# Feed-forward: the stores of the down projection's right factors move from SyncE's DMA queue to GpSimd's

## The chip, the core and the metric

The program runs on one core of a Trainium2 chip. A core has TensorE (PE: matrix products; a weight load PEld goes beside it), VectorE (DVE), ScalarE (ACT), GpSimd (POOL) and SyncE (SP), and 16 DMA engines that move data between its on-chip memory (SBUF) and DRAM. The engines run apart from each other. Each takes its own instructions strictly in order and waits, where told, on counters that other engines and finished transfers raise. A DMA is issued by an engine as one instruction in that engine's order. Here nearly all are issued by SP, which computes nothing.

The metric is the device time of one execution in microseconds (us); less is better. It is given as the median of several runs. The profile is one further execution, recorded by the hardware.

## The reference

One inference step of a two-layer decoder in fp32. A prompt of 1024 tokens, 16 learned meta tokens and 8 x 8 sampled tokens go through together, 1104 rows of width 1024. Layer 0 is a Mamba-2 mixer and a feed-forward block, layer 1 a sliding-window attention and a feed-forward block, then a final norm. What matters here is the feed-forward block, which is there once in each layer:

```python
hn = rmsnorm(h, ffn_norm_g[layer])
h = h + (silu(hn @ w_gate[layer]) * (hn @ w_up[layer])) @ w_down[layer]   # 1024 -> 2816 -> 1024
```

## The kernel before

**Seven products for eight.** Each feed-forward product is done by Strassen's scheme in Winograd's form. Both factors are cut into 2 x 2 blocks, sums and differences of the blocks are formed, and seven block products take the place of eight. `PRODUCTS` names for each product its left factor (A11, A12, A22, S1 to S4, from the weights) and its right factor (B11, B21, B22, T1, T2, T3, N4, from the activations). Each factor is split into a high and a low part (`split_copy`, L78 to L80: ACT writes the rounded high part H, L79, and DVE the rest L, L80), and `mm` (L1489 to L1493) makes one product of three matmuls: H by xH, H by xL, L by xH.

**Up.** `up` runs over 22 slices `j` of 128 gate and up columns. Each slice has seven products of 24 matmuls (each 128 x 128 by 276 columns in layer 0, 272 in layer 1). `after_up` (L1495 to L1532) takes each finished product out of PSUM: on ACT (L1500, L1509) and on DVE (L1507, L1510, L1512, L1514, L1516, L1520), and joins them to silu(gate) times up.

**The right factors for down.** Two slices make a unit `u`, 11 in all. Each unit gives seven right factors of [128, 2, 552] in layer 0 and [128, 2, 544] in layer 1 (high and low part), which do not fit on the chip. `task` (L1534) makes a small function for each: a difference on DVE where one is needed (L1540), the split into one of three staging buffers taken in turn (L1541 to L1543: ACT's L79, DVE's L80), and a DMA that stores the staging buffer to its DRAM tile `facts[u][nm]` (L1544). That is 77 stores in each layer. The staging buffers lie in memory called `big` (layer 0) or `hN` (layer 1), two of them, and `tot`, the third; the DRAM tiles show as `f_B`, `f_T` and `f_N`, by the factor's first letter. While the up products run, one task is taken per product (L1456 and L1457); the tasks left at the end are taken during the first two products of down (L1628).

**Down.** `down` (L1568) goes through the units in chunks of two, the last of three, with seven products each, in the first chunk in the order B11, T2, T3, N4, B21, T1, B22 (`DOWN_FIRST`). `load` (L1574 to L1588) fetches the right factors back from DRAM into six buffers `bo`, as early as a buffer is free (L1585). These lie over the memory of the right factors of up: the first `bo` buffer over T2 of up, the others over T2 and T3, so that the first load waits in the instruction stream for up's last read of T2 and the second for its last read of T3. The left factors come from `prepare_down`: `source` forms S1, S3, S2 and S4 on DVE (L1131, L1134, L1138, L1141) and `factor` splits them (ACT L1149, DVE L1150). In the first product of the first chunk PE goes over unit 0 for all four row blocks, 24 matmuls, and then over unit 1. The results are added to the residual `hN` (DVE, L1639); where a lane is new they are copied to `sumX`, `sumY` or `sumZ` (ACT, L1649). The residual itself is fetched back from DRAM (`res`) into `hN` when product index 2 to 5 of the whole stage begins (L1608), over memory that the last tasks still read.

**What sets the order.** The text of the program gives each instruction a place. A planner then walks a model of the machine and lays down each engine's order once, ahead of time: what is ready first on the model is put first. SP's order thus holds weight loads (L1170 for gate and up, L1181 for down), the stores L1544, the loads L1585 and the residual's loads L1608, in the order in which they came up on the model; on the chip an instruction that isn't ready holds up all that follow it in its queue. The order of each queue around the change is planned anew when the store changes its queue.

Of the kernel before, what the change touches and what calls it, by code (L numbers as in the profile page):

```python
# [10 lines left out]
F32 = mybir.dt.float32  # L11
# [66 lines left out]
def split_copy(nc, H, L, src):  # L78
    nc.scalar.copy(H, src)  # L79
    nc.vector.tensor_tensor(L, src, H.bitcast(F32), ALU.subtract)  # L80
# [1129 lines left out]
class FeedForward:  # L1210
# [323 lines left out]
    def task(self, u, nm, at, terms=None):  # L1534


        def run():
            nc = self.nc
            if terms:
                nc.vector.tensor_tensor(at, *terms, ALU.subtract)  # L1540
            st = self.stage[self.turn % 3]  # L1541
            self.turn += 1
            split_copy(nc, st[:, 0], st[:, 1], at)  # L1543
            nc.sync.dma_start(self.facts[u][nm][:], st.bitcast(F32))  # L1544

        self.tasks.append(run)

# [936 lines left out]
```

## Time and profile before

| | |
|---|---|
| median of 3 runs | 2869.57 us (2868.34 to 2872.6) |
| the profiled execution, its own time | 2869.85 us |
| its span, first to last instruction | 2868.1 us |
| PE, DVE, ACT, POOL busy | 2760.2, 2022.5, 1222.4, 487.1 us |
| feed-forward of layer 0: stores L1544 | 1052.1 to 1489.0 us |
| the same of layer 1 | 2196.0 to 2623.7 us |
| stores L1544, by SP | 154 |

Engine rows give the busy time of each engine. A row of the timeline gives start, length, engine, line, operation and tiles, and in brackets how long the engine stood idle before it and what ended that. "issue" there means that the profile shows nothing for which the engine waited. A row of a window table gives a stretch, its length, and then for PE, PEld, DVE, ACT and POOL the busy time and the count of instructions, the granted TensorE clock (1.00 is full), the busy share of the DMA engines and the GB/s that they moved. SPq marks SP's queue: the time at which it issued, not the time of the transfer; a row with x2 or x4 runs from the first issue to the end of the last.

### The profile page before, as it was taken

What the parts mean: (1) busy time and instruction counts of PE and PEld (TensorE: products, weight loads), DVE (VectorE), ACT (ScalarE), POOL (GpSimd) and SP (SyncE); (2) the same over time, 40 slices, a digit from 0 to 9 for tenths busy, and PEclk for the clock granted to TensorE, in tenths of its full rate; (3) what the DMA queues carried; (4) which work ended last, traced back from release to release, by engine and by line L of the source; (5) the groups of instructions that cost most, each with busy time, mean ns of one, the idle gap of its engine ahead of it and who ended that gap; (6) DMA issues with size and microseconds to landing.
All of it is one profiled execution on the core that took longest, in us unless ns stands there. A gap on an engine that the chain in (4) does not pass through costs nothing. (4 is left out here: it accounts for less than half of the span.)

```text
span 2868.1 us, 51222 instructions
## 1 busy us (share of the span) xinstructions
PE 2760.2 (96%) x19990; PEld 2545.5 (89%) x19990; DVE 2022.5 (71%) x3633; ACT 1222.4 (43%) x2580; POOL 487.1 (17%) x692
## 2 busy tenths in 40 slices
PE   7999999899999899999999999998999999999998
PEld 7888989877888799999999997665998999999998
DVE  6779676647574698777768791555479777877786
ACT  4667554346442344333332243545434433433224
POOL 1455444314222100000000002332210000000000
PEclk9999999999999999999999999998999999999999
DMA  6776866565554434444468652001623443437664
GB/s 201 236 233 225 273 216 215 183 234 192 198 177 169 137 99 171 136 150 140 138 258 305 227 198 79 20 23 50 184 88 114 171 136 131 161 142 303 239 219 156
DMA packets 327009, 496.58 MB, mean 173 GB/s; under 512 B 24479, under 2 KB 222559, under 8 KB 325713
## 3 DMA queue, kind: packets, MB, share of 16 engines
q1 hardware_dynamic: 325614, 491.20, 50.5%
q8 instruction: 158, 2.59, 0.4%
q10 hardware_dynamic: 1152, 2.10, 0.2%
q14 instruction: 85, 0.70, 0.1%
HBM read 317.93 MB, written 175.30 MB: 172 GB/s over the span
## 5 line engine op out<-in xcount | busy, mean ns | idle before, releaser
L1149 ACT CAST wo<-ws 128x512 fp32r<-128x512 f32 x428 | 263.7, 620 | 546.1 <-PE wacc L1492 246.5
L1491 PE MATMUL dacc<-bo,wo 128*128 128x276 f32 (+1 forms) x1232 | 360.3, 292 | 10.3 <-DMA bo<-f_B 5.4
L1493 PE MATMUL dacc<-bo,wo 128*128 128x276 f32 (+1 forms) x1232 | 358.0, 291 | 0.0
L1492 PE MATMUL dacc<-bo,wo 128*128 128x276 f32 (+1 forms) x1232 | 357.9, 291 | 0.0
L1150 DVE TENSOR_TENSOR wo<-ws,wo 128x512 fp32r<-128x512 f32 x428 | 297.4, 698 | 69.0 <-ACT wo L1149 59.6
L73 PE MATMUL acc<-uH,wH 128*128 128x296 f32 (+1 forms) x840 | 276.5, 329 | 1.7 <-DVE th L762 1.6
L74 PE MATMUL acc<-uL,wH 128*128 128x296 f32 (+1 forms) x840 | 275.5, 328 | 0.0
L75 PE MATMUL acc<-uH,wL 128*128 128x296 f32 (+1 forms) x840 | 274.2, 326 | 0.9 <-DVE wL L156 0.9
L1491 PEld LDWEIGHTS dacc<-bo,wo 128*128 128x128 f32 x1232 | 234.4, 190 | 11.5 <-issue 10.9
L1492 PEld LDWEIGHTS dacc<-bo,wo 128*128 128x128 f32 x1232 | 234.4, 190 | 0.0
L1493 PEld LDWEIGHTS dacc<-bo,wo 128*128 128x128 f32 x1232 | 234.1, 190 | 0.0
L73 PEld LDWEIGHTS acc<-uH,wH 128*128 128x128 f32 x840 | 158.9, 189 | 16.7 <-issue 6.6
L75 PEld LDWEIGHTS acc<-uH,wL 128*128 128x128 f32 x840 | 158.8, 189 | 11.6 <-issue 2.3
L74 PEld LDWEIGHTS acc<-uL,wH 128*128 128x128 f32 x840 | 158.8, 189 | 10.6 <-issue 2.2
L585 DVE SCALAR_TENSOR_TENSOR cc<-raw,convw,cc 128x616 f32<-128x616 f32 (+1 forms) x144 | 134.3, 936 | 39.5 <-ACT cc L583 37.9
L1639 DVE TENSOR_TENSOR hN<-hN,dacc 128x544 f32<-128x544 f32 (+1 forms) x164 | 116.7, 720 | 27.9 <-PE dacc L1493 26.4
L73 PE MATMUL acc<-yH,wH 128*128 128x296 f32 (+1 forms) x360 | 122.3, 342 | 6.9 <-ACT yH L79 3.7
L2285 POOL MEMSET mask<- 128x64 f32 x1 | 0.2, 154 | 727.0 <-PE dacc L1493 727.0
L74 PE MATMUL acc<-yL,wH 128*128 128x296 f32 (+1 forms) x360 | 120.6, 336 | 0.1
L75 PE MATMUL acc<-yH,wL 128*128 128x296 f32 (+1 forms) x360 | 120.2, 335 | 0.0
L1491 PE MATMUL wacc<-N4H,wo 128*128 128x276 f32 (+1 forms) x352 | 102.7, 292 | 4.7 <-DVE hN L1504 2.4
L1149 ACT CAST wo<-sum 128x512 fp32r<-128x512 f32 x66 | 41.0, 622 | 154.3 <-PE wacc L1492 106.7
(594 smaller groups left out, 8615.3 us busy)
## 6 DMA issues: line engine op xcount, KB each, us to landing
kept<-wH SPq DMA_DIRECT2D x56, 512.0 KB
kept<-wL SPq DMA_DIRECT2D x56, 512.0 KB
ws<-ffn_w_gate SPq DMA_DIRECT2D x44, 512.0 KB
ws<-ffn_w_up SPq DMA_DIRECT2D x44, 512.0 KB
ws<-ffn_w_down SPq DMA_DIRECT2D x44, 512.0 KB
ws<-ssm_w_in SPq DMA_DIRECT2D x40, 512.0 KB
wH<-kept SPq DMA_DIRECT2D x38, 512.0 KB
wL<-kept SPq DMA_DIRECT2D x38, 512.0 KB
```

The lines of the kernel that those rows point to most:

```text
L73: nc.tensor.matmul(out, wH, xH, start=start, stop=False)
L74: nc.tensor.matmul(out, wH, xL, start=False, stop=False)
L75: nc.tensor.matmul(out, wL, xH, start=False, stop=stop)
L585: nc.vector.scalar_tensor_tensor(o, raw[:, k : k + n], w(k), o, ALU.mult, ALU.add)
L1149: nc.scalar.copy(H, src)
L1150: (low or nc.vector).tensor_tensor(L, src, H.bitcast(F32), ALU.subtract)
L1491: nc.tensor.matmul(out, wH, xH, start=start, stop=False, skip_group_check=True)
L1492: nc.tensor.matmul(out, wH, xL, start=False, stop=False, skip_group_check=True)
L1493: nc.tensor.matmul(out, wL, xH, start=False, stop=stop, skip_group_check=True)
L1639: add = lambda d, s: nc.vector.tensor_tensor(d, d, s, ALU.add)
L2285: nc.gpsimd.memset(A.mask0[:, :NS], NEG)
```

## The change

The store of a staged right factor is issued by GpSimd in place of SyncE. Nothing else is edited. The same 154 transfers move the same bytes between the same places; only the queue in which the instruction stands, and the way in which its transfer is set up, are others.

```diff
             st = self.stage[self.turn % 3]
             self.turn += 1
             split_copy(nc, st[:, 0], st[:, 1], at)
-            nc.sync.dma_start(self.facts[u][nm][:], st.bitcast(F32))
+            nc.gpsimd.dma_start(self.facts[u][nm][:], st.bitcast(F32))
```

## The prediction

> **What bounds the kernel now.** I read the page first, then busy time by stretches, then PE's timeline where it is not full, then the queue or engine that ends last there.
>
> ```profile
> span 2868.1 us, 51222 instructions
> PE 2760.2 (96%) x19990; PEld 2545.5 (89%) x19990; DVE 2022.5 (71%) x3633; ACT 1222.4 (43%) x2580; POOL 487.1 (17%) x692
> ```
>
> ```profile
> 1300.00:1400.00 100.00, 100.00 (x787) 100.00 (x786) 79.92 (x125) 39.20 (x66) 0.00 (x0) 1.00 0.46 158
> 1400.00:1500.00 100.00, 94.99 (x721) 94.39 (x720) 67.37 (x104) 39.87 (x67) 0.00 (x0) 0.97 0.55 202
> ```
>
> PE bounds it. While the up products run and stores go out, PE is full (first row), so nothing that only speeds SP's queue there can gain. The change can gain only where PE stands idle near a store. That is the turn from up to down, twice in each layer:
>
> ```profile
> 1467.52 0.29 PE L1491 MATMUL dacc<-bo,wo 128*128 128x276 f32 x1
> ...
> 1473.53 0.57 PE L1491 MATMUL dacc<-bo,wo 128*128 128x276 f32 x1 [2.79 <-DMA bo<-f_B]
> ...
> 1499.85 0.41 PE L1491 MATMUL dacc<-bo,wo 128*128 128x276 f32 x1 [2.04 <-issue]
> ...
> 2609.75 0.56 PE L1491 MATMUL dacc<-bo,wo 128*128 128x272 f32 x1 [2.62 <-DMA bo<-f_B]
> ...
> 2635.09 0.36 PE L1491 MATMUL dacc<-bo,wo 128*128 128x272 f32 x1 [2.67 <-issue]
> ```
>
> The clock is cut after some of these, which costs as well:
>
> ```profile
> 1440.00:1445.00 5.00, 5.00 (x41) 5.00 (x40) 3.63 (x6) 0.83 (x2) 0.00 (x0) 1.00 0.41 161
> ...
> 1460.00:1465.00 5.00, 4.82 (x38) 4.59 (x37) 1.79 (x3) 0.00 (x0) 0.00 (x0) 1.00 0.01 3
> ...
> 1470.00:1475.00 5.00, 2.21 (x12) 2.02 (x12) 5.00 (x9) 0.97 (x2) 0.00 (x0) 0.77 0.99 351
> 1475.00:1480.00 5.00, 5.00 (x26) 5.00 (x25) 5.00 (x9) 5.00 (x11) 0.00 (x0) 0.54 0.80 329
> ...
> 1500.00:1505.00 5.00, 5.00 (x28) 5.00 (x29) 3.81 (x7) 0.73 (x1) 0.00 (x0) 0.66 1.03 406
> ```
>
> ```profile
> 2610.00:2615.00 5.00, 5.00 (x31) 5.00 (x32) 5.00 (x10) 4.38 (x10) 0.00 (x0) 0.72 1.02 420
> ```
>
> Full clock gives 41 matmuls in 5 us, one in 0.122; half clock one in 0.245. The 26 of the fourth row mean half clock up to about 1478.6, 5.1 us after PE resumed, a loss of 2.6 us. In the same way I read losses of 1.6 us at 1500 and 1.3 us at 2610, and next to none after 2635. So the four stalls cost 5.4 + 3.6 (layer 0) and 3.9 + 2.7 (layer 1): **15.6 us in all, the most that can be won**.
>
> **Why PE waits.** SP's queue in layer 0, then the first rows of layer 1:
>
> ```profile
> 1455.82 0.39 SPq L1585 DMA_DIRECT2D bo<-f_B  x1
> 1467.64 0.32 SPq L1544 DMA_DIRECT2D f_B<-big  x1
> 1468.06 0.38 SPq L1585 DMA_DIRECT2D bo<-f_B  x1
> 1468.53 2.56 SPq L1585 DMA_DIRECT2D bo<-f_T  x4
> 1471.21 8.54 SPq L1585 DMA_DIRECT2D bo<-f_N  x2
> ...
> 1489.02 0.63 SPq L1544 DMA_DIRECT2D f_B<-big  x1
> 1489.70 1.08 SPq L1608 DMA_DIRECT2D hN<-res  x2
> ```
>
> ```profile
> 2603.78 0.52 SPq L1544 DMA_DIRECT2D f_B<-hN  x1
> 2604.39 0.56 SPq L1585 DMA_DIRECT2D bo<-f_B  x1
> ...
> 2607.50 7.20 SPq L1585 DMA_DIRECT2D bo<-f_N  x2
> ```
>
> The second load of `bo` (unit 1's B11) stands behind a store that isn't ready until 1467.6. By itself it waits only for up's last read of T3, which is over when DVE can take that product out:
>
> ```profile
> 1460.52 0.73 DVE L1512 TENSOR_TENSOR hA<-big,wacc 128x552 f32<-128x552 f32 x1 [3.60 <-PE wacc L1493]
> ...
> 1475.76 0.68 DVE L1150 TENSOR_TENSOR wo<-ws,wo 128x512 fp32r<-128x512 f32 x1
> ...
> 1477.01 0.68 DVE L1150 TENSOR_TENSOR wo<-ws,wo 128x512 fp32r<-128x512 f32 x1
> ...
> 1499.03 1.36 DVE L1639 TENSOR_TENSOR hN<-hN,dacc 128x552 f32<-128x552 f32 x2
> ```
>
> ```profile
> 2613.07 0.68 DVE L1150 TENSOR_TENSOR wo<-ws,wo 128x512 fp32r<-128x512 f32 x1
> ...
> 2634.27 3.46 DVE L1639 TENSOR_TENSOR hN<-hN,dacc 128x544 f32<-128x544 f32 x5 [0.55 <-DMA hN<-res]
> ```
>
> So the store holds the loads for 7.5 us, in which the DMA engines are idle (share 0.01 above). The second stall of each layer ends when DVE can add the fourth product to the fetched residual (L1639 at 1499.03 and 2634.27, PE 0.8 us later); the residual's load was issued at 1489.70 into full DMA engines and took 9.3 us.
>
> **The change, part by part.** *Removed from SP*: 154 issues of 0.32 to 0.52 us and their waits. In up they lie beside a full PE: 0.
>
> *Added on POOL*: 154 issues. No row shows a DMA issued by POOL. Lower bound 0.32 us (SP's rows); upper bound 1.63, the longest single POOL instruction on the chain of waits:
>
> ```profile
> 2122.20 1.63 POOL tot L2211
> ```
>
> ```profile
> L2285 POOL MEMSET mask<- 128x64 f32 x1 | 0.2, 154 | 727.0 <-PE dacc L1493 727.0
> ```
>
> I take 1 us, between the two. POOL has nothing to do for 727 us around layer 0's stores, so nothing is queued behind them; in layer 1 it has only two tiny memsets for the final norm. Cost on the path 0, at either end. What a slower landing could delay is the reuse of a staging buffer three tasks later, which rival C prices.
>
> *First stall, layer 0.* The second load goes at about 1460.5 and the four behind it follow. Their size:
>
> ```profile
> bo<-f_B SPq DMA_DIRECT2D x33, 552.0 KB
> ...
> hN<-res SPq DMA_DIRECT2D x4, 1104.0 KB
> ```
>
> Five of 0.565 MB at 351 GB/s take 8 us, so all are in by 1469 and PE's first product ends 48 x 0.122 after 1467.52, at 1473.4, not at about 1479.2 (24 x 0.122 at mixed clock after 1473.53, as above). But what is late next? The second product needs S2's low parts, and these come from DVE, which is busy 5.00 of 5 us from 1470 to 1480: unit 0's is done at 1476.4, unit 1's at 1477.65. DVE's chain starts with the end of up and doesn't wait for the loads, so it does not move. Eight matmuls can run before the last of these and 40 after it: end at 1477.65 + 4.9 = 1482.6, plus a cut of the clock, since PE stands idle some 3 us again. The four stalls above lost 0 to 2.6 us by it, 1.4 in the mean; so 1484.0 against 1479.2 + 5.9 = 1485.1. **Gain 1.1 us of the 5.4** (bounds -0.1 to 2.5).
>
> *First stall, layer 1.* PE's first product ended at about 2614.1 (the `f_N` row ends its wait there), the second at 2620.0. Afterwards: unit 1's low part at 2613.7, plus 4.9, plus 1.4: 2620.0. **Gain 0** (bounds -1.2 to 1.4).
>
> *Second stalls.* The residual's load no longer has a store of 0.63 us before it, and 2.8 MB of loads have left the DMA engines 7 us sooner. Bounds of its landing: at the soonest its issue plus its own 1.13 MB at 351 GB/s, 1489.7 + 3.2 = 1492.9; at the latest as before, 1499.0. DVE adds 0.8 us later. I take half of the 7 us: it lands at 1495.5, DVE's add is there at 1496.3, and PE, which ends the fourth product at 1484.0 + 2 x 5.9 = 1495.8, stands for 0.5 us, too short for a cut: **gain 3.1 us of 3.6**. In layer 1 the same step brings the landing to 2630.8, ahead of PE at about 2632: **gain 2.7** (bounds of both: 0 to all).
>
> Sum: 1.1 + 0 + 3.1 + 2.7 = 6.9 us. Against the profiled execution (2869.85 us, 1.75 of it outside the span) that makes 2863.0; it stands 0.3 above the median of 2869.57. **Predicted: 2862.7 us**, 0.24% faster, own range 2857 to 2867, from the bounds of the two first stalls and a part of the two second ones.
>
> The Trainium skill has a rule against this change ("DMA: Bandwidth & Descriptors", Issuing engines are not separate DMA queues): DMAs of all issuing engines run on the same 16 engines, and another issuer saves only sequencer issue time, usually small. By that rule alone the result is 2869.6; the row at 1467.64 speaks for more, as SP there lost a wait of 11 us ahead of ready loads, not an issue of 0.32.
>
> **Rivals.** *A, nothing moves* (2868 to 2871): DVE takes the place of the first waits, and the residual still lands late, because stores and loads now share the DMA engines side by side from 1478 on. For it: share 0.80 to 1.03 from 1470 on. Against: the idle DMA time at 1460.
>
> *B, all is won* (2869.6 - 15.6 = 2854.0): the planner, with another queue in its model, puts DVE's S2 ahead. For it: the order is planned anew. Against: S2's inputs are the same, and DVE is full there.
>
> *C, slower: late staging buffers.* Landing through POOL is so much later that the split three tasks on waits, and DVE and ACT with it.
>
> ```profile
> 1435.65 1.61 SPq L1544 DMA_DIRECT2D f_T<-big  x2
> ...
> 1441.73 0.32 SPq L1544 DMA_DIRECT2D f_B<-big  x1
> ```
>
> ```profile
>   ACT big L79: 6.5, 5
>   ACT tot L79: 3.8, 2
> ```
>
> The tightest reuse is 6.1 us from store to store, of which the two passes of the split take 1.5 (0.73 each, like the row at 1460.52): a store may take 4.6 us to land. ACT already waited for stores 7 times in layer 0 while PE was full. The same engines must take a finished product out of PSUM within one product of 24 x 0.122 = 2.9 us, a pass included, so PE stops from a landing of 4.6 + 2.2 = 6.8 us on. At 7.5 us each of the 20 units after the first ones would cost 0.7, 14 us in all: 2877 with the 6.9 won; at 8.5 us 2897. The Trainium skill names a cause ("SBUF — State Buffer", Who interferes with whom): descriptors written by GpSimd are held up while VectorE runs a two-port operation. By it nothing would be lost here, since it excepts operations with two tensor inputs, and every DVE row above is one; no run here shows it yet.
>
> **How the numbers follow.** Chances: forecast 0.46, A 0.23, B 0.14, C 0.17. What this kernel's times can tell apart is about 0.2%, 5.7 us, so faster means below 2863.8. Of the forecast's own range six tenths lie below that, 0.28; with B faster is 0.42. The other 0.18 and A make same 0.41. C is slower, 0.17. Range: the forecast and A whole, B from just above its price, C up to its nearer price: 2855 to 2877, which leaves out most of B and the far half of C.
>
> **What would show it.** Right: the second `bo` load issued near 1460; PE's first idle stretch moved from the middle of the first product to the start of the second, waiting for `wo` from DVE; no PE stall when the residual lands; POOL busy with about 154 issues. Wrong: ACT's waits for `f_` stores grown to many us and PE below full between 1050 and 1450 (C); the 2.0 and 2.7 us stalls still there (A); PE full through both turns (B).

## The result, and the profile after

The changed kernel takes 2881.32 us in the median of 7 runs (2877.14 to 2890.01), the kernel before 2869.51 (7 runs, 2868.29 to 2872.71). The ratio is 1.0040, 95% interval 1.0026 to 1.0053: **slower by 11.8 us, 0.4%**. Forecast were 2862.7 us and a range of 2855 to 2877, so the sign and the range were wrong.

The profiled execution of the changed kernel is its longest run, 2890.01 us. Its page begins:

```profile
span 2888.2 us, 51263 instructions
PE 2774.8 (96%) x19990; PEld 2557.4 (89%) x19990; DVE 2023.2 (70%) x3633; ACT 1220.9 (42%) x2580; POOL 577.0 (20%) x846
```

**Where the time went.** Four places divide the span: ACT's first and last copy out of an up product in each layer (L1500), and the first matmul `pS` of the attention (L1077). Before, then after (start of the first and of the last of each group):

```profile
L1500 ACT COPY big<-wacc x19: 612/620/624, 1063.7 to 1446.6; 128x552 f32<-128x552 f32 x19
L1500 ACT COPY hN<-wacc x19: 609/613/616, 2206.8 to 2583.0; 128x544 f32<-128x544 f32 x19
...
L1077 PE MATMUL pS<-cmask_sb,tot x18: 165/250/250, 1717.6 to 1742.3; 128*128 128x1 f32 x16, 128*80 128x1 f32 x2
```

```profile
L1500 ACT COPY big<-wacc x19: 608/619/623, 1069.4 to 1452.4; 128x552 f32<-128x552 f32 x19
L1500 ACT COPY hN<-wacc x19: 607/612/615, 2219.3 to 2595.4; 128x544 f32<-128x544 f32 x19
...
L1077 PE MATMUL pS<-cmask_sb,tot x18: 165/250/251, 1727.5 to 1752.2; 128*128 128x1 f32 x16, 128*80 128x1 f32 x2
```

Up takes 382.9 us before and 383.0 after in layer 0, and 376.2 and 376.1 in layer 1: nothing is lost there. From the last copy of up to `pS` (below: turn 0) it is 271.0 before and 275.1 after; from the last copy in layer 1 to the end of the span (turn 1) 285.1 and 292.8. That is 4.1 + 7.7 = **11.8 us in the two turns** of this profile. That it equals the difference of the medians is in part chance: in a second profile of the same kernel, below, the turns are longer by 6.7 us, since fewer stalls there are followed by half clock. What the profiled run is longer by beside the turns (5.7 us ahead of the first up copy, 2.6 in the attention) belongs to that run: in the second profile the attention takes 487.0 us, less than the 489.2 before.

**In up the stores are free.** Windows of the changed kernel inside up, and the answer of its trace on the store's line L1544 (durations in ns, minimum, median, maximum):

```profile
1300.00:1400.00 100.00, 100.00 (x787) 100.00 (x785) 77.94 (x121) 40.16 (x67) 8.53 (x16) 1.00 0.43 138
...
2500.00:2600.00 100.00, 100.00 (x801) 100.00 (x800) 76.56 (x120) 39.53 (x65) 12.09 (x19) 1.00 0.44 150
```

```profile
L1544 POOL DMA_DIRECT2D f_B<-big x23: 531/531/562, 1058.8 to 1494.1; - x23
L1544 POOL DMA_DIRECT2D f_B<-hN x23: 667/676/695, 2209.2 to 2636.3; - x23
...
  ACT tot L79: 0.6, 3
  ACT hN L79: 0.2, 1
```

PE is full. One issue costs POOL 0.53 us in layer 0 and 0.68 in layer 1, and ACT waited four times for a store, 0.8 us together. A list of the DMA issues gives the time from issue to landing as a median of 3.0 to 4.6 us.

**In the turns PE now stops three times, not twice.** PE's rows with idle time, layer 0 and then layer 1:

```profile
1482.73 0.60 PE L1491 MATMUL dacc<-bo,wo 128*128 128x276 f32 x1 [3.17 <-ACT sumX L1649]
...
1504.77 0.37 PE L1491 MATMUL dacc<-bo,wo 128*128 128x276 f32 x1 [2.04 <-issue]
...
1520.85 0.57 PE L1491 MATMUL dacc<-bo,wo 128*128 128x276 f32 x1 [3.64 <-issue]
...
2623.11 0.39 PE L1491 MATMUL dacc<-bo,wo 128*128 128x272 f32 x1 [0.54 <-ACT sumX L1649]
...
2647.45 0.57 PE L1491 MATMUL dacc<-bo,wo 128*128 128x272 f32 x1 [3.09 <-issue]
...
2665.53 0.36 PE L1491 MATMUL dacc<-bo,wo 128*128 128x272 f32 x1 [3.19 <-issue]
```

```profile
1476.00:1481.00 5.00, 3.56 (x28) 3.34 (x27) 5.00 (x10) 1.22 (x3) 0.00 (x0) 1.00 0.53 154
1481.00:1486.00 5.00, 3.27 (x14) 3.27 (x15) 5.00 (x9) 5.00 (x11) 0.79 (x2) 0.66 0.33 131
...
1521.00:1526.00 5.00, 5.00 (x22) 5.00 (x23) 3.06 (x5) 1.45 (x2) 0.00 (x0) 0.50 1.01 397
```

The first stall of layer 0 has moved from the middle of the first product to the start of the second, as forecast. But its row does not name the left factor from DVE for which PE was forecast to wait: it names ACT's copy of the first product out of PSUM (`sumX`). ACT's rows, and the DVE row of unit 0's low part:

```profile
1480.40 0.62 ACT L1149 CAST wo<-ws 128x512 fp32r<-128x512 f32 x1 [0.63 <-DVE ws L1138]
...
1482.07 0.61 ACT L1649 COPY sumX<-dacc 128x552 f32<-128x552 f32 x1
```

```profile
1481.51 0.69 DVE L1150 TENSOR_TENSOR wo<-ws,wo 128x512 fp32r<-128x512 f32 x1
```

The low part is done at 1482.2, the copy at 1482.7, and PE starts at 1482.73. The first product ended about 1479.6; its copy stands in ACT's order behind a cast that waits for DVE's differences (L1138). So DVE's chain still sets the stall, by way of ACT and PSUM.

The second stall is there still, at the same length in layer 0 and 0.4 us longer in layer 1; the third (3.64 and 3.19 us, and in layer 0 half clock behind it, the 22 matmuls of the window's last row) is new. What stands around it in the queues, SP first, before and after, then DVE, before and after:

```profile
1501.66 1.72 SPq L1608 DMA_DIRECT2D hN<-res  x2
1503.48 1.70 SPq L1181 DMA_DIRECT2D ws<-ffn_w_down  x2
```

```profile
1457.70 8.75 SPq L1585 DMA_DIRECT2D bo<-f_B  x2
...
1476.53 3.38 SPq L1585 DMA_DIRECT2D bo<-f_N  x2
1489.81 1.08 SPq L1585 DMA_DIRECT2D bo<-f_B  x2
...
1494.15 0.85 SPq L1608 DMA_DIRECT2D hN<-res  x2
...
1505.85 0.81 SPq L1181 DMA_DIRECT2D ws<-ffn_w_down  x2
1507.63 0.80 SPq L1608 DMA_DIRECT2D hN<-res  x2
```

```profile
1511.95 2.00 DVE L1639 TENSOR_TENSOR hN<-hN,dacc 128x552 f32<-128x552 f32 x3
1513.87 0.68 DVE L1150 TENSOR_TENSOR wo<-ws,wo 128x512 fp32r<-128x512 f32 x1
1514.47 0.72 DVE L1639 TENSOR_TENSOR hN<-hN,dacc 128x552 f32<-128x552 f32 x1
```

```profile
1517.01 0.69 DVE L1150 TENSOR_TENSOR wo<-ws,wo 128x512 fp32r<-128x512 f32 x1 [0.50 <-ACT wo L1149]
1517.62 0.68 DVE L1134 TENSOR_TENSOR ws<-ws 128x512 f32<-128x512 f32 x1
1518.22 0.69 DVE L1150 TENSOR_TENSOR wo<-ws,wo 128x512 fp32r<-128x512 f32 x1
1518.82 1.29 DVE L1141 TENSOR_TENSOR ws<-ws 128x512 f32<-128x512 f32 x2
1520.03 2.64 DVE L1639 TENSOR_TENSOR hN<-hN,dacc 128x552 f32<-128x552 f32 x4
```

Two orders have changed. In SP's queue two loads of `w_down` (512 KB each) now go ahead of the second half of the residual (`hN<-res`, the load at 1507.63), which they followed before. In DVE's queue the four additions into that half (L1639 at 1520.03), which make PSUM free for PE, stand behind six passes for left factors of later products (the rows above, and one L1131 at 1515.82); before, five of the six came behind all four additions and one between the third and the fourth. Nobody edited either order. The second half of the residual overwrites the memory in which the last store's factor is staged, so its load must follow that store; when the store changed its queue, the planner put the load, and the additions that need it, later in the orders. On the chip layer 0's load goes at the same time after up's last copy as before (55.2 us against 55.1); what is different is the 1 MB of `w_down` ahead of it.

### The profile page after: what moved, and what is told of

Its sections match the earlier page's. It is cut to its first block, busy times and chain, and to the rows that moved or that the text cites. A ratio compares the mean times of both kernels' runs of the same rounds, so it can differ in the third digit from the quotient of the medians.

```text
span 2888.2 us, 51263 instructions
## 1 busy us (share of the span) xinstructions
PE 2774.8 (96%) x19990; PEld 2557.4 (89%) x19990; DVE 2023.2 (70%) x3633; ACT 1220.9 (42%) x2580; POOL 577.0 (20%) x846
## 4 chain that ended last, share of the span: by engine, by line
PE 80%; DVE 7%; ACT 2%; issue 1%; DMA 1%; POOL 1%; SPq 0%; DVEq 0%; ACTq 0%; POOLq 0%
PE wacc L1491 10%; PE wacc L1493 10%; PE wacc L1492 10%; PE acc L73 6%; PE acc L74 6%; PE acc L75 6%; PE dacc L1491 5%; PE dacc L1493 5%; PE dacc L1492 5%; PE pP L73 2%; PE pP L74 2%; PE pP L75 2%; PE ps L670 1%; ACT work L2096 1%; PE ps L667 1%
## 5 line engine op out<-in xcount | busy, mean ns | idle before, releaser
L75 PEld LDWEIGHTS acc<-uH,wL 128*128 128x128 f32 x840 | 159.5, 190 | 10.7 <-issue 2.3
L1639 DVE TENSOR_TENSOR hN<-hN,dacc 128x544 f32<-128x544 f32 (+1 forms) x164 | 116.9, 722 | 34.5 <-PE dacc L1493 33.7
L1491 PE MATMUL wacc<-B11H,wo 128*128 128x276 f32 (+1 forms) x352 | 104.4, 297 | 2.6 <-ACT sqh L1060 2.6
L1491 PE MATMUL wacc<-T2H,wo 128*128 128x276 f32 (+1 forms) x352 | 102.4, 293 | 4.2 <-ACT T2H L79 4.2
```

Source lines behind the costliest of these rows:

```text
L75: nc.tensor.matmul(out, wL, xH, start=False, stop=stop)
L1491: nc.tensor.matmul(out, wH, xH, start=start, stop=False, skip_group_check=True)
L1639: add = lambda d, s: nc.vector.tensor_tensor(d, d, s, ALU.add)
```

## Experiments

Turn 0 and turn 1 of each profiled run, PE's second stall and the longest one behind it in layer 0 and layer 1 (us; a dash where PE did not stop for 0.5 us), and the ratio of times to the kernel before, with its 95% interval:

| kernel | turn 0 | turn 1 | second stall | later stall | ratio |
|---|---|---|---|---|---|
| before | 271.0 | 285.1 | 2.04, 2.67 | -, - | 1 |
| changed | 275.1 | 292.8 | 2.04, 3.09 | 3.64, 3.19 | 1.0040 (1.0026 to 1.0053) |
| a1_again | 274.1 | 288.7 | 2.38, 3.09 | 3.69, 3.19 | 1.0039 (1.0027 to 1.0051) |
| a3_tail_pool | 274.6 | 290.5 | 2.61, 3.09 | 3.65, 3.19 | 1.0037 (1.0023 to 1.0051) |
| a4_b22_sp | 269.5 | 283.5 | 2.88, 2.05 | -, - | 0.9998 (0.9990 to 1.0007) |
| a7_act | 269.9 | 290.6 | 2.00, 1.99 | -, 4.25 | 1.0026 (1.0016 to 1.0036) |
| a8_clean | 268.8 | 286.5 | 2.04, 2.03 | -, 1.24 | 1.0006 (0.9997 to 1.0016) |
| f1_dve | 271.1 | 285.2 | 2.04, 3.09 | 2.17, - | 1.0014 (1.0005 to 1.0023) |
| e4_b21_pool | 270.4 | 283.7 | 2.04, 2.03 | -, - | 1.0002 (0.9992 to 1.0012) |
| e1_bytes | 273.1 | 288.0 | 5.45, 3.69 | -, - | 1.0025 (1.0015 to 1.0035) |
| f3_first_half | 267.9 | 286.5 | 2.06, 2.61 | -, - | 1.0003 (0.9993 to 1.0014) |
| f4_b21_first_half | 268.0 | 284.7 | 1.38, 1.40 | 1.24, - | 0.9996 (0.9987 to 1.0005) |
| b6_stage4 | 268.1 | 284.6 | -, 1.28 | 2.18, 1.03 | 0.9994 (0.9986 to 1.0003) |
| w1_b21_stage4 | 268.3 | 284.0 | -, 1.28 | 1.21, 1.47 | 0.9994 (0.9985 to 1.0004) |
| d2_clean_stage4 | 271.5 | 287.9 | -, 0.86 | 2.37, 2.71 | 0.9999 (0.9988 to 1.0010) |
| d1_force_stage4 | 268.5 | 285.3 | -, - | 1.82, 1.81 | 1.0006 (0.9997 to 1.0016) |
| e2_b21_order | 271.3 | 283.3 | 2.04, 2.03 | 1.14, - | 0.9993 (0.9984 to 1.0002) |

Each turn is read from one profile, and half clock follows a stall in one profile and not in another, so that turns of one kernel differ by 1 to 4 us (the rows of changed and a1_again). The quoted expectations end turn 0 up to 0.3 us sooner, at the weight load ahead of `pS`.

Up takes 382.9 or 383.0 us in layer 0 and 375.9 to 376.2 in layer 1 in every one of them, with 154, 152, 8, 2 or no stores on POOL, or with 154 on ACT.

### Is the loss in the turns, and does it hold?

a1_again is the changed kernel once more.

> The changed kernel once more. Theory O (order): all of the loss, 2881.3 - 2869.5 = 11.8 us, lies in the two turns from up to down, 4.2 us in layer 0 (from the last ACT copy of up at 1446.6 / 1452.4 to the first product of the attention at 1717.3 / 1727.3) and 7.7 us in layer 1 (from the last such copy at 2583.0 / 2595.4 to the end of the span); the 8.2 us by which the first profile is longer elsewhere (6.0 of them before any store of the change is issued) belong to that one execution. So: a median of 2877 to 2883, a third PE stall of 3 to 4 us in each layer, and a profile whose stretches outside the turns are within 2 us of the kernel before. Rival R (the rest): the other stretches are longer by 6 us again, and the change costs something before its first store.

Its median is 2881.08 us. Its profiled run is the shortest of its 6 (2877.65 us), with the same third stalls:

```profile
1480.42 0.40 PE L1491 MATMUL dacc<-bo,wo 128*128 128x276 f32 x1 [3.17 <-ACT sumX L1649]
...
1517.49 0.57 PE L1491 MATMUL dacc<-bo,wo 128*128 128x276 f32 x1 [3.69 <-issue]
```

Its first up copy comes at 1067.1, 3.4 us later than before; the runs below have it anywhere from 1063.7 to 1070.8, whatever their stores. Outside the turns this run is 1.1 us longer than before (3.4 - 2.2 in the attention - 0.1), inside them 6.7. The first profile's 7.7 us of layer 1 are partly the cut clock: 4.1 of them are not here, with the same stalls. Ahead of the last 15 us of the span PE has half clock three times there (from 2626.0, 2646.5 and 2667.0, 13.7 us together), here once (from 2653.2, 3.4 us).

### Which stores make it?

```diff
+            tail = u == self.nj // 2 - 1 and nm in ("T2", "T3", "N4", "B22")
-            nc.gpsimd.dma_start(self.facts[u][nm][:], st.bitcast(F32))
+            (nc.gpsimd if tail else nc.sync).dma_start(self.facts[u][nm][:], st.bitcast(F32))
```

> Only the last four stores of each layer (T2, T3, N4, B22 of unit 10) go to GpSimd's queue, the other 73 stay with SyncE. Theory O: the loss comes from the last store alone: with it in another queue the planner puts two 512 KB loads of w_down in SyncE's queue ahead of the second half of the residual. That order is the same here, so the third stall (3.6 and 3.2 us, with the cut clock after it 6 and 5 us) is back in both layers while the 1.1 us of the first stall are not won: 2880 to 2885. Rival S (sharing): the loss comes from the 150 other stores, which share the DMA engines with the loads from a second queue; then this kernel is within 2 us of 2869.5 and shows no third stall.

And the reverse: all on GpSimd but the last store of each layer.

```diff
+            last = u == self.nj // 2 - 1 and nm == "B22"
-            nc.gpsimd.dma_start(self.facts[u][nm][:], st.bitcast(F32))
+            (nc.sync if last else nc.gpsimd).dma_start(self.facts[u][nm][:], st.bitcast(F32))
```

> All stores go to GpSimd's queue but one in each layer: B22 of unit 10, the last, stays with SyncE. Theory O: the planner puts the second half of the residual ahead of the two w_down loads again, as before the change, and there is no third stall in either layer: the loss is gone, and the 1 us of the first and second stalls of layer 0 may be left as a gain: 2866 to 2871. Rival S: 75 of 77 stores of a layer are unchanged against the slow kernel, so the time stays at 2877 to 2883.

Four stores of 77 give the whole loss (2880.91 us), and one store back on SP takes all of it away (2868.71 us; PE's first stall in layer 0 below). So that store decides where the planner puts the second half of the residual, at least together with the three ahead of it: the last store alone on GpSimd was not run. The other 76 stores, POOL's issues, its landings and the sharing of the DMA engines cost nothing that shows (0.9998, 0.9990 to 1.0007).

```profile
1479.09 0.40 PE L1491 MATMUL dacc<-bo,wo 128*128 128x276 f32 x1 [3.17 <-ACT sumX L1650]
```

### Is it GpSimd?

```diff
-            nc.gpsimd.dma_start(self.facts[u][nm][:], st.bitcast(F32))
+            nc.scalar.dma_start(self.facts[u][nm][:], st.bitcast(F32))
```

> All stores go to ScalarE's queue instead of GpSimd's. The planner's order then has the second half of the residual ahead of w_down in layer 0 and behind it in layer 1. Theory O: a third stall in layer 1 (about 3 us and the cut clock after it, 5 us in all) and none in layer 0. Rival G (GpSimd): what costs is the way GpSimd's transfers are set up or land (median 3.0 to 4.6 us from issue to landing, 10.0 at most); then neither layer shows a third stall. Either way ScalarE stands at each issue until VectorE has finished the split, 1.5 us x 154 at most in its own idle time, which may cost PE some us in the up phase: 2872 to 2895 in all; the verdict rests on the two turns, not on the sum.

The planner gave this kernel the old orders in layer 0 and the late ones in layer 1, and PE stops at the third place in layer 1 alone. Its rows there, SP's, then DVE's, then PE's:

```profile
2631.56 2.55 SPq L1181 DMA_DIRECT2D ws<-ffn_w_down  x2
2634.15 0.91 SPq L1608 DMA_DIRECT2D hN<-res  x2
```

```profile
2648.12 0.69 DVE L1141 TENSOR_TENSOR ws<-ws 128x512 f32<-128x512 f32 x1
2648.72 2.61 DVE L1639 TENSOR_TENSOR hN<-hN,dacc 128x544 f32<-128x544 f32 x4
```

```profile
2649.54 0.57 PE L1491 MATMUL dacc<-bo,wo 128*128 128x272 f32 x1 [4.25 <-issue]
```

So the loss goes with the orders, within one kernel and without any DMA on GpSimd.

### SP's order or DVE's?

a8_clean leaves every store on GpSimd and only orders SP's queue at one place, the two later `w_down` loads behind the second half of the residual.

```diff
+        self.first = []
...
                     nc.sync.dma_start(hN[e][:, fs], self.saved[e][:, fs])
+                    if e:
+                        self.units.first.append(nc.cur_bb.bb.instructions[-1])
...
             self.nc.sync.dma_start(t[:], w)
+            if self.first:
+                self.first.append(self.nc.cur_bb.bb.instructions[-1])
...
+                if i == 7:
+                    in_order(tc, self.units.first[:2] + self.units.first[4:], nc.sync)
+                    self.units.first = []
```

> As the changed kernel, all 154 stores on GpSimd's queue, but the order in SyncE's queue is fixed at one place in each layer: the two loads of w_down that came ahead of the second half of the residual come behind it. Theory O (the order alone): no third stall in either layer; the turns take about 269.5 us in layer 0 and 283.5 in layer 1, as in the run with only the last store on SyncE, and the time is 2867 to 2872. Rival L (landing): the second half of the residual overwrites the staging buffer of the last store and so waits until that store has landed, up to 10 us after GpSimd issues it; then the third stall stays at 2 to 4 us whatever the order, the turns take 273 to 275 and 288 to 291, and the time is 2877 to 2883.

The third stall is gone in layer 0; in layer 1 a wait of 1.24 us for a left factor from ACT stands in its place. Rival L falls: the load still has to wait for the last store on POOL, and that costs nothing that shows. The median, 2873.69 us, lies 1.7 us above the range expected; by the interval of the ratio it can't be told from the kernel before. But the planner moved DVE's additions too: they stand ahead of the six passes again. f1_dve tells the two orders apart. SP's order stays as the change made it; only the six DVE passes are put behind the additions (`prep` stands wherever `down` called `next(self.prep)`).

```diff
+        traced, adds, later = nc.cur_bb.bb.instructions, [], []
+        def prep():
+            n = len(traced)
+            next(self.prep)
+            if adds:
+                later.extend(x for x in traced[n:] if x.engine == nc.vector.engine)
...
                     self.after_down(XYZ, c, p, mi, ps[:, 512 - q : 512 + q], final)
+                    if i == 5:
+                        adds.append(traced[-1])
...
+                if i == 16:
+                    for x in (later[j] for j in (6, 7, 22, 24, 30, 31)):
+                        in_order(tc, [adds[-1], x], nc.vector)
```

> The changed kernel, all 154 stores on GpSimd's queue and SyncE's queue in the order that the change gave it (two loads of w_down ahead of the second half of the residual). Only VectorE's order is fixed at one place in each layer: six passes for later left factors (sums and low parts, about 4 us) that the changed kernel has ahead of the four additions into the second half of the residual come behind these, as most of them did before the change. Theory D (VectorE's order: its queue is served in order, and the additions that free PSUM stand behind passes that nobody waits for): no third stall, or below 1 us, in either layer; turns of 268 to 271 and 283 to 287 us, 2867 to 2874. Theory O in its first form (SyncE's order: the residual lands late behind w_down): VectorE now stands idle until the residual has landed, PE's third stall stays at 3 to 4 us in both layers, turns of 274 and 289 us, 2877 to 2883.

2874.59 us. Here L1652 is the addition, L1639 of the kernel before:

```profile
1520.05 2.65 DVE L1652 TENSOR_TENSOR hN<-hN,dacc 128x552 f32<-128x552 f32 x4 [2.65 <-DMA hN<-res]
```

```profile
1520.88 0.36 PE L1491 MATMUL dacc<-bo,wo 128*128 128x276 f32 x1 [2.17 <-issue]
```

Both orders count. In layer 1 the third stall is gone: there DVE's order was all of it. In layer 0 2.17 of 3.6 us are left, and now DVE stands idle for 2.65 us until the residual, behind `w_down` in SP's queue, has landed 10.7 us after its issue (1509.31). By the ratios DVE's order makes 1.0039 - 1.0014, some 7 us, and SP's order 1.0014 - 1.0006, some 2 us; their intervals of about 3 us to either side leave the second open, and SP's order alone, with DVE's left late, was not run.

### What the change was to win: the first stall

e4_b21_pool moves one store of each layer to GpSimd, the one behind which the second load stood.

```diff
+            held = u == self.nj // 2 - 1 and nm == "B21"
-            nc.sync.dma_start(self.facts[u][nm][:], st.bitcast(F32))
+            (nc.gpsimd if held else nc.sync).dma_start(self.facts[u][nm][:], st.bitcast(F32))
```

> The kernel before, with one store of each layer moved to GpSimd's queue: B21 of unit 10, behind which the second right factor of the down phase stood in SyncE's queue (issued at 1467.64). The order of SyncE's queue is otherwise that of before. Theory H (this one store is all that the change could win): the first stall moves to the start of the second product in both layers, the second stays at 2 to 3 us, there is no third; the turns take 269 to 270 and 283 to 284 us as in the run that kept only the last store on SyncE, and the time is 2865 to 2870. Rival (the gain of those turns came from the other 75 stores): the first stall stays as before, 270.7 and 285.1 us.

The first stall moves in both layers, as with all 154 stores: these two stores are enough for it. Turns 0 and 1 are 0.6 and 1.4 us shorter than before in this profile. That this is all that the change could win is not shown: the median is 2869.50 us, and a gain of 2 us is less than its interval (0.9992 to 1.0012) can tell.

### Why the second stall stayed

By the prediction it ends when the first half of the residual lands, behind the loads in full DMA engines. e1_bytes adds bytes ahead of it, in the kernel before.

```diff
+                    if i == 2:
+                        for x in range(2):
+                            nc.sync.dma_start(self.spare[x][:], self.facts[4 + x]["B11"][:])
+                            self.stored.append(nc.cur_bb.bb.instructions[-1])
                     nc.sync.dma_start(hN[e][:, fs], self.saved[e][:, fs])
+                    if i == 2:
+                        in_order(tc, self.stored[-3:] + [nc.cur_bb.bb.instructions[-1]], nc.sync)
```

> The kernel before, with work added: in each layer SyncE's queue gets two copies of an old right factor into a spare DRAM buffer (2 x 0.56 MB) between the last store and the first half of the residual. Theory B (the bytes ahead of the residual in the full DMA engines set PE's second stall): 1.13 MB at 400 GB/s are 2.8 us, so the stall grows from 2.04 to about 4.8 us in layer 0 and from 2.67 to about 5.5 in layer 1, and the time by 5 to 9 us with the cut clock behind longer stalls: 2875 to 2880. Rival V (VectorE's work, or the wait for its last split, sets it, and the residual would land in time): both stalls stay within 0.5 us and the time within 2 us.

```profile
1500.20 2.65 DVE L1648 TENSOR_TENSOR hN<-hN,dacc 128x552 f32<-128x552 f32 x4 [3.32 <-DMA hN<-res]
```

```profile
1501.03 0.57 PE L1493 MATMUL dacc<-bo,wo 128*128 128x276 f32 x1 [5.45 <-issue]
```

The stalls grow by 3.4 and 1.0 us (2.8 each were expected), the time by 0.25%. Not all of the 3.4 comes from the bytes: with no half clock behind its first stall, PE ends the fourth product of layer 0 2.3 us sooner here. Counted from ACT's last copy of up, the second stalls end 1.1 and 0.9 us later than before. The first half lands 11.7 us after its issue at 1488.54. Bytes ahead of the residual count, then, though by less than was expected. But in the kernel before DVE's row at 1499.03 shows no wait. Right ahead of it stands this one:

```profile
1497.66 1.45 DVE L1150 TENSOR_TENSOR wo<-ws,wo 128x512 fp32r<-128x512 f32 x2 [1.58 <-ACT wo L1149]
```

Two passes for a later product, which begin when ACT's casts are done; in the program these casts take a buffer that PE's running product gives back. f3_first_half puts these two behind the additions; nothing else is edited.

```diff
+                    if i == 3:
+                        adds.append(traced[-1])
...
+                if i == 8:
+                    for x in (later[5], later[7]):
+                        in_order(tc, [adds[-1], x], nc.vector)
```

> The kernel before, SyncE's queue unchanged; only in VectorE's queue two passes of each layer (the low parts of two left factors for a later product, 1.45 us, whose ScalarE casts wait for PE's running product) come behind the four additions into the first half of the residual instead of ahead of them. Theory D (PE's second stall of 2.0 us is VectorE's order: PE's product, then the cast, then these passes, then the additions that free PSUM): the stall goes or falls below 1 us in layer 0, and falls by about 0.5 to 2 us in layer 1, where the residual itself came 0.55 us after the passes; the row of the additions then shows when the residual really lands. 2865 to 2869. Theory of the prediction (the residual's landing ends the stall): VectorE stands idle until the landing, and the stalls stay at 2.0 and 2.7 us: 2868 to 2872.

```profile
1496.81 2.65 DVE L1652 TENSOR_TENSOR hN<-hN,dacc 128x552 f32<-128x552 f32 x4 [2.99 <-DMA hN<-res]
```

```profile
1497.59 0.39 PE L1491 MATMUL dacc<-bo,wo 128*128 128x276 f32 x1 [2.06 <-DVE hN L1652]
```

The stalls stay (2.06 and 2.61), and DVE now idles until the residual lands, 9.3 us after its issue at 1487.52. So the prediction's reading was right, and theory D of that expectation is wrong for the second stall: the landing sets it, and DVE's two passes end close by. (Turn 0 is 3.1 us shorter in this profile, which has no half clock in layer 0; the ratio of times is 1.0003.) With the first stall out of the way, f4_b21_first_half, the same edit on e4_b21_pool:

> The same in the kernel with only B21 of unit 10 on GpSimd's queue (turns of 270.1 and 283.7 us). PE ends the fourth product 1 to 2 us sooner there, so more of the stall may be the residual itself. Theory D: the second stall falls from 2.0 to between 0 and 1.5 us in both layers, the turns to 268 to 269 and 282 to 283, and the time to 2864 to 2868. By the residual's landing: both stalls stay at 2 us or more, and the time at 2867 to 2870.

The stalls fall from 2.04 and 2.03 to 1.38 and 1.40, so the passes seem to have cost the 0.6 between in e4_b21_pool; the landing itself does not show there. The landing came 9.0 us after the issue in both layers (1488.94 to the next row in layer 0).

```profile
1497.90 2.65 DVE L1653 TENSOR_TENSOR hN<-hN,dacc 128x552 f32<-128x552 f32 x4 [2.93 <-DMA hN<-res]
```

### Versions that could beat both

In the program the first half's load can't go ahead of DVE's last split, and that split waits until T2's store has left its staging buffer. b6_stage4 gives the last factor a fourth buffer, all stores on SP.

```diff
             st = self.stage[self.turn % 3]
+            if u == self.nj // 2 - 1 and nm == "B22":
+                st = self.x1[:, 2:4].bitcast(F32R)
```

> The kernel before, all stores on SyncE, but the last factor of each layer (B22 of unit 10) is split into a fourth staging buffer (rows 2 and 3 of the same tile, free by then), not into the one that T2's store has to leave first. Theory W (what holds the first half of the residual is VectorE's last split, and that waits for T2's store): the residual's first load goes some 4 to 7 us sooner than 1489.7, PE's second stall (2.0 and 2.7 us, 3.6 and 2.7 with the clock) goes or falls below 1 us in both layers, and the time falls by 3 to 6 us, to 2863 to 2867. Rival B (bytes): the DMA engines are full from 1485 on, so a load that goes sooner only pushes back the right factors of the next product; the stall changes its name and the time stays at 2868 to 2872.

The load goes 35.3 us after ACT's last copy of up (1484.06), not 43.1 us (1489.70 before), and the second stall is gone in layer 0 and halved in layer 1. In its place PE waits for a right factor:

```profile
1512.43 0.36 PE L1491 MATMUL dacc<-bo,wo 128*128 128x276 f32 x1 [2.18 <-DMA bo<-f_B]
```

Both theories had a part: the load went sooner, as W said, and the loads behind it came later, as B said. The same buffer with e4's store (w1_b21_stage4), and with all stores on GpSimd and the order of a8_clean (d2_clean_stage4), or with all four `w_down` loads behind both halves (d1_force_stage4: the same lists without the slice `[:2]` and `[4:]`):

> Two parts that each won something in one turn, together: B21 of unit 10 on GpSimd's queue (turns of 270.1 and 283.7 us against 270.7 and 285.1) and the fourth staging buffer for the last factor (267.9 and 284.6); all other stores on SyncE. If the gains add, the turns take 267 and 283 us, 6 us less than before, and the time is 2863 to 2866. If the first stall, now won, only moves to the right factors of the next product (as the fourth buffer alone showed at 1512), the turns take 269 to 271 and 284 us: 2867 to 2870.

> All stores on GpSimd's queue, the fixed order (second half of the residual ahead of the two w_down loads) and the fourth staging buffer for the last factor together. Theories O and W: no third stall, no second stall, and the 1 to 1.5 us per layer of the first stall won: 2869.5 - 3.1 - 6.3 = 2860 at the best, 2860 to 2865. Rival B: no third stall, but the second one stays or moves: 2865 to 2870.

> As the run before it, but all four loads of w_down that stood around the residual come behind both of its halves, so that 1.05 MB less (2.6 us at 400 GB/s) stand ahead of the first half. If bytes in the DMA engines set the second stall (rival B), it falls by up to 2.6 us in each layer against the run before it, and the time by 2 to 6 us. If VectorE's last split sets it (theory W), nothing more is won by this, and w_down, which is now late, may hold VectorE's sums for the eighth product: 0 to 6 us slower than the run before it.

w1_b21_stage4 has the shortest turns of all, 3.8 us below the kernel before, and a median of 2869.47 us. d2 took 2869.47 and d1 2873.36 us: the second stall falls, and later ones of 1.8 to 2.7 us come instead. e2_b21_order is e4 with the `w_down` loads fixed behind the first half:

```diff
                     nc.sync.dma_start(hN[e][:, fs], self.saved[e][:, fs])
+                    if not e:
+                        self.units.first.append(nc.cur_bb.bb.instructions[-1])
...
+                    in_order(tc, self.units.first, nc.sync)
```

> As the run with B21 of unit 10 on GpSimd's queue, and the four loads of w_down of that stretch fixed behind the first half of the residual, so that 1.05 MB less stand ahead of it. Theory B: the residual lands up to 2.6 us sooner and the second stall (2.0 to 2.9 us, and the cut clock) goes or nearly goes in both layers: 2861 to 2866. Against it: VectorE's sums then get w_down late, and PE stands for wo one or two products later by about as much: 2866 to 2871.

2867.86 us, with the second stalls unchanged at 2.04 and 2.03 though 1.05 MB less stand ahead in the queue; DVE's two passes are ahead of the additions here, so the residual's landing is hidden, and this run doesn't tell what it did. No version is faster than the kernel before by more than its interval.

## Why the prediction was wrong, step by step

*PE bounds it, and up hides 154 issues on either engine*: right. Up is unchanged to 0.1 us. An issue on POOL costs 0.53 or 0.68 us, where 1 was taken.

*First stall*: right in its cause, about its size, and wrong in what is late next. The held load goes when up's last read allows it, and PE ends the first product unbroken. Then it waits 3.17 us, not for the second product's left factor but for ACT's copy of the first product out of PSUM; the left factor's low part is there 0.5 us sooner. The prediction had no term for that copy, and its sum held because both hang on the same chain of DVE. From ACT's last copy to the end of the fourth product (second stall's row less its idle time) it is 1499.85 - 2.04 - 1446.6 = 51.2 us before, 50.3 in the first profile after and 49.0 in the second: 0.9 and 2.2 us won, 1.1 forecast. In layer 1 it is 49.4 before, 49.0 and 47.5 after: 0.5 and 2.0, where 0 was forecast. That 0.9 comes near 1.1 is partly luck: in layer 0 half clock followed the stall in the first profile and not in the second.

*Second stalls*: wrong, 5.8 us forecast and none won. The step took half of the 7 us by which the loads ahead go sooner as time won at the residual's landing. But the residual's issue hangs on DVE's last split, not on the store, and the DMA engines had nothing more to do in the time set free: their share is 0.53 and 0.33 from 1476 to 1486, since the next two loads wait for a `bo` buffer that the second product holds (the issue at 1489.81). They were nearly full again when the residual came (0.86 from 1490 to 1495, then 0.99). It landed 10.1 us after its issue in the second profile (1490.45 to 1500.54, where DVE waits 0.25 us for it); before, at most 9.3.

*POOL's stores cost 0 on the path, at either end*: wrong, and this is **the step that lost the sign**. It looked at what stands behind a store on POOL and on SP, and kept every other order of before. Behind the last store stands the second half of the residual, through the memory and not through a queue. Put at 0, the term measured a third stall of 3.64 us in layer 0 and 3.19 in layer 1, with half clock behind them, and made the kernel 11.8 us slower; with the old orders and the same 154 stores on POOL (a8_clean, 1.0006, 0.9997 to 1.0016) no loss is left that its interval can tell. The chance for a new plan was given to rival B, as a gain.

*The rivals*: A's picture (the second stall stays, since the landing does not move) came true, but not its time. C had the right sign for the wrong place: ACT waited for stores for 0.8 us in all, and landings of 3.0 to 4.6 us in the median do not exceed the 4.6 that it worked out as bearable. What slowed the kernel none of them named. The rule of the Trainium skill that the prediction weighed against the change ("DMA: Bandwidth & Descriptors", Issuing engines are not separate DMA queues: another issuer saves only issue time) agrees with these runs as to the gain: 152 stores on GpSimd without the loss (a4_b22_sp) make 0.9998 of the time before. The loss of 11.8 us came with the orders of the queues, on which it says nothing.

What stays open: why the planner's model puts the residual so late when the last store is on another queue was not looked into; the runs show only that it does, on POOL in both layers and on ACT in one.

## What to carry to other kernels

Where a planner lays down the queues, an edit to one DMA's queue is an edit to all orders: look for who waits for the moved transfer through memory (here a load that overwrites its source), and compare the orders of every engine around that point before pricing the edit. An addition or copy that makes PSUM free belongs ahead of passes for later products in an in-order queue; six short passes ahead of it cost PE 3.2 us in layer 1. A load that is taken off a wait wins only if the next resource in its chain (a buffer, an engine, the DMA engines) is free at that time.

## What the hardware showed that was not expected

**The same stall costs a different time from run to run.** Behind the first stall of 3.17 us the first profile after has half clock (0.50 from 1482.55 to 1486.0), the second has none (1.00 from 1480 to 1490). The first matmul alone doesn't tell: after 2665.53 it took 0.36 us, and half clock began 1.4 us later. In all 17 profiles each stretch of half clock in the turns, up to the last 15 us of the span, lasts 3.4 us or 6.8, so each costs up to 1.7 or 3.4 us of matmul time, and profiles of one kernel differ by several us in a turn (292.8 and 288.7). The Trainium skill has a reason ("TensorE: Matmul & The Clock Gate", Part 1: The HAM clock gate): the gate looks at windows of about 3.4 us that run freely, so that what a stall costs depends on where it falls in them. These traces agree: in the first profile after, half clock begins at 1482.55, 1520.10, 2626.00, 2646.45 and 2666.95, and the distances from the first are 11, 335, 341 and 347 times one length, 3.413 us (1184.40 / 347). That a whole idle window is needed does not agree: half clock follows the stall of 2.79 us in the kernel before, and at 2626.00 stops of only 0.54, 0.67 and 0.19 us. In the profiles of the kernel before and the two of the changed one, the ten stretches of 3.4 us that end where half clock begins hold 2 to 12 matmuls, where full rate gives 28; stretches of the same grid with a stop and no half clock behind it hold 12 or more. The prediction took a stop of 0.5 us as too short for a cut; no length alone decides it here.

**A load of 1.13 MB took 9 to 11 us** from its issue (9.3, 9.0 and 10.7 us above) where 351 GB/s alone would make 3.2, as the DMA engines were full (share near 1.0) with what had been issued ahead; with 1.13 MB more ahead of it (e1_bytes) it took 11.7.
